# One encoder layer: result stores on ScalarE's and GpSimd's queues, three larger result tiles, and h2 blocks stored without norm_mlp's factors

## The chip, the cores and the metric

The kernel runs on one core of a Trainium2 chip. The time is the device time of one execution in microseconds (us). TensorE (PE) does the matmuls, with PEld for its weight loads; VectorE is DVE, ScalarE is ACT, GpSimd is POOL, and SyncE (SP) issues DMAs. Each of them works through its own list of instructions in order.

## The reference

One layer of an encoder: a norm, an input projection, two kinds of attention, gates and an output projection, and a feed-forward part with squared ReLU, all in fp32, for 2048 tokens of 1024 features.

```python
h = rms_norm(x, norm_mix[l])
z = h @ w_in[l]                      # 1024 x 4352
q_a, k_a, v_a, q_b, k_b, v_b, g_a, g_b = jnp.split(z, offsets, axis=-1)
y_a = windowed_gqa(...)              # |t-s| <= 128, ALiBi, sink
y_b = neighborhood_attn(...)         # 8 x 16 window on a grid of 64 columns
y = sigmoid(g_a + b) * (y_a @ w_proj_a) + sigmoid(g_b + b) * (y_b @ w_proj_b)
x = x + y @ w_out
h2 = rms_norm(x, norm_mlp[l])
x = x + relu(h2 @ w_up) ** 2 @ w_down
...
return rms_norm(x, norm_final)
```

## The kernel before, in words

Every fp32 operand of a large product is split into a high and a low part (a cast by ACT, a subtraction by DVE: L280 and L281), and a product is three matmuls, high x high, high x low, low x high (L200 to L202, L284 to L286). The large projections go in *quads*: two blocks of tokens by two blocks of features, computed with seven block products in place of eight, so operands and results pass through sums and differences on DVE (L277).

The program has these stages, in the order of time of the profile:

- **Input projection, up to about 380 us.** Nine quads (QUADS, L548). `in_quad` and `in_seeded` evict the results of each product from PSUM into tiles of the ring `zc` (ten tiles of 128x512) or, for q and k, as high and low part into the ring `ze` (two tiles of 128x2x512). `in_result` (L440) stores them: q and k to `qs_*` and `ks_*` (L450), v to `vs_*` (L458), the gates to `zg` (L461). All go on SP's queue.
- **Beside it, the parts of W_out.** In the third, fourth, eighth and ninth quad, a generator `wo_parts` (L663 to L690) makes the seven sums of W_out's blocks, splits each into `hi` (a `zc` tile) and the low part (in place, in a `zv` or `xin` tile), and stores both to `wo_d` (L677). One step of it runs after each product of the quad (`next(prep)`, L723). In the sixth and seventh quad two blocks of normalised x are transposed by DVE into `ze` tiles and stored to `h1d` (`turned_out`, L239).
- **Windowed attention A (about 380 to 700 us)**, which reloads `h1d` (`h_pages`, L743: `raw<-h1d`, four loads a block, hT by ACT and DVE) for the q, k and v of the last two blocks of tokens. It needs the table `dist` (L793), from which POOL makes the bias tiles `biasa` (L799), and loads of `ka`, `va`, `qa`.
- **Neighbourhood attention B (about 700 to 1075 us).**
- **Gated projection and W_out (about 1075 to 1410 us)**: `gated` and `out_products`; the parts of W_out come back as `pgl<-wo_d`. The results are normalised rows; `turned_out` transposes them, multiplies by norm_mlp's factors (`gain`, L252) and stores four pieces of 32x8x128 for each of four groups to `h2d`. Blocks 0 and 1 go through `ht` tiles earlier; blocks 2 and 3 come last, through the two tiles `m` and the four tiles `hu` (`turned_last`, L1456).
- **Up projection (about 1410 to 2030 us)**: `up_right` makes the seven right-hand pages (`ubh1` to `ubh7`) of h2, `ahead` and `parts_ahead` prepare those of the second half (blocks 2 and 3) in small chunks, `up_quad` does the products. The pages lie where tiles of the stage before lay, so a page waits until `m` or `hu` is stored.
- **Down projection and the final norm, to the end.**

Nearly every DMA is on SP's queue, in program order: 1364 rows of SP's list. A DMA whose data is not ready, whose target is not free, or whose semaphore (eight are shared in turn by the DMAs of SP and ACT) is still in use holds up all behind it. Before the change POOL issues no DMA, and ACT 48 (32 of `zg`, in the attention, and 16 of `x2d`). The order on each engine is made by a scheduler from the program's dependences, so an edit in one place also shifts rows elsewhere.

Of the kernel before, what the change touches and what calls it, by code (L numbers as in the profile page):

```python
# [8 lines left out]
F32 = mybir.dt.float32  # L9
F32R = mybir.dt.float32r  # L10
AF = mybir.ActivationFunctionType
# [81 lines left out]
def encoder_layer(ctx, tc, x, norm_mix, w_in, b_gate, sink, rpb, w_pa, w_pb, w_out,  # L93
# [12 lines left out]
    def pools(stack, side, tags, name):  # L106

        return {t: pool(f"{name}_{t}", side=side, stack=stack) for t in tags}
# [130 lines left out]
    def turned_out(d, ht, tiles, g, gain=None, queue=None):  # L239

        hv = ht.rearrange("p (j t c) -> p t j c", j=8, t=4)
        for t in range(4):
            V.transpose(out=hv[:, t], in_=tiles[t][:, g * 256 : (g + 1) * 256].rearrange("p (j c) -> p j c", j=8))
        h3 = ht.rearrange("p (j x) -> p j x", j=8)
        if gain is not None:
            (step, n), _ = gain.ap  # L250
            gv = bass.AP(gain.tensor, gain.offset + 8 * g, [[step, n], [1, 8], [0, P]])
            V.tensor_tensor(out=h3, in0=h3, in1=gv, op=ALU.mult)  # L252
        dv = d.rearrange("(j i) (a x) -> a i j x", i=32, a=4)
        for a in range(4):
            (queue or SY).dma_start(dv[a][:, 8 * g : 8 * g + 8], h3[32 * a : 32 * a + 32])
# [36 lines left out]
    def ring(stack, tag, shape, dt, bufs, side="right"):  # L292

        pl = pool(f"r_{tag}", side=side, stack=stack)
        return lambda: T(pl, shape, dt, tag, bufs)
# [25 lines left out]
    in_sum = ring(s_z, "zS", [P, 4, 256], F32, 2)  # L321
    in_v2 = [ring(s_z, "zv2", [P, 1024], F32, 1)]
    in_page[5] = ring(s_z, "zh5", PAGE, F32R, 2)
    in_c = ring(s_z, "zc", [P, BT], F32, 10)
    in_e = ring(s_z, "ze", [P, 2, BT], F32, 2)
    in_whl = ring(s_z, "zwhl", [P, 2, 4, 256], F32R, 3)
    in_page[3] = ring(s_z, "zh3", PAGE, F32R, 2)
    s_kv = ExitStack()
# [117 lines left out]
    def in_result(col, b, src, in_psum):  # L446

        if col < O_VB and col != O_VA:
            for dst, t in qk_parts(col, b, src, in_e()):
                SY.dma_start(dst, t)  # L450
            return
        if in_psum:
            t = in_c()
            A.copy(t, src)
            src = t
        if is_v(col):
            for dst, t in v_parts(col, b, src, zbank(tpool, 2), in_v2[-1]()):
                SY.dma_start(dst, t)  # L458
        else:
            f = (col - O_GA) // P  # L460
            SY.dma_start(zg[b][0][f // 8, (f % 8) * P : (f % 8 + 1) * P, :], src)  # L461

    def in_quad(c, w, lf, right, ybanks=ypool, zbanks=zpool):

# [198 lines left out]
    def wo_parts(k, own):  # L663

        rows = [own(), own()]
        for p, r in enumerate(rows):
            SY.dma_start(r, w_out[0][(4 * p + k) * P : (4 * p + k + 1) * P, :])
        yield
        b11, b12, b21, b22 = (r[:, j * BT : (j + 1) * BT] for r in rows for j in range(2))
        t1, t3 = (t[:, j * BT : (j + 1) * BT] for t in (own(),) for j in range(2))  # L670

        def part(n, src):
            hi = in_c()
            A.copy(hi.bitcast(F32R), src)
            V.tensor_tensor(out=src.bitcast(F32R), in0=src, in1=hi, op=ALU.subtract)
            for z, t in enumerate((hi, src)):
                SY.dma_start(wo_d[n][k // 2, k % 2][:, z], t)  # L677

        add(V, t1, b12, b11, ALU.subtract)
        yield  # L680
        add(V, t3, b22, b12, ALU.subtract)
        part(1, b11)
        yield
        add(V, b12, b22, t1, ALU.subtract)
        part(3, b22)
        yield
        add(V, b11, b21, b12, ALU.subtract)
        for n, src in ((2, b21), (5, t1), (7, t3), (6, b12), (4, b11)):
            part(n, src)
            yield  # L690
# [9 lines left out]
    for q in range(2, len(QUADS)):  # L700
        prep = iter(())
        if q in (2, 3):
            prep = wo_parts(q - 2, own_v)
        elif q in (7, 8):
            prep = wo_parts(q - 5, own_x)
        next(prep, None)
        if q == 5:
            s_v.close()
            in_v2.pop()
            xp = pools(s_z, "right", ("xin", "st"), "x2")  # L710
        if q == 7:
            bias_tables()
        lf = list(in_left(ws, 256, (1, 2) if q == 2 else (), ORDER if q == 2 else ORDER_3))
        if q + 1 < len(QUADS):
            ws = in_weights(*QUADS[q + 1])
        if q in (5, 6):

            b = q - 3
            xt = x_tiles(xp, b, 3)
            normalised(xp, xt, Junk(), by_scalar=True)  # L720
        ops2.extend(lf if q == 2 else ())
        for n, _ in enumerate(quad2 if q == 2 else in_seeded(*QUADS[q], iter(lf), right)):
            next(prep, None)  # L723
            if q in (5, 6) and n < 4:
                turned_out(h1d[b - 2], in_e().rearrange("p k x -> p (k x)"), xt, n)
        for _ in prep:
            pass
# [388 lines left out]
    p4x["st"] = cp  # L1116
    gain = turned_gain(T(p4x, [P, P], F32, "gt", 1), norm_mlp)
    next(first_y)

    n_bank = [0]  # L1120

# [76 lines left out]
    h2p_d = {n: [dp.tile([BT, BT], F32, name=f"h2part{n}{z}") for z in range(2)] for n in (1, 5)}  # L1198
    stored = [None]

    def parts_ahead(n):

        src = h2d[2] if n == 1 else h2s_d[n]
        for k in range(4):
            lo, hi = up_rings["chunk"](), up_rings["chunk"]()
            with tc.issue_after(stored[0]) if k == 0 and stored[0] else nullcontext():
                SY.dma_start(lo, src[k * P : (k + 1) * P, :])
            yield
            A.copy(hi.bitcast(F32R), lo)
            V.tensor_tensor(out=lo.bitcast(F32R), in0=lo, in1=hi, op=ALU.subtract)  # L1210
            for z, t in enumerate((hi, lo)):
                SY.dma_start(h2p_d[n][z][k * P : (k + 1) * P, :], t)

    def ahead(k):

        b = {}
        for j, p in ((0, 0), (1, 0), (1, 1), (0, 1)):
            b[p, j] = up_rings["chunk"]()
            with tc.issue_after(stored[0]):
                SY.dma_start(b[p, j], h2d[2 + j][p * BT + k * P : p * BT + (k + 1) * P, :])  # L1220
        t1, t3, t2, t4 = b[0, 0], b[0, 1], b[1, 1], b[1, 0]
        for n, out, x, y in ((5, t1, t3, t1), (7, t3, t2, t3), (6, t2, t2, t1), (4, t4, t4, t2)):
            yield
            add(V, out, x, y, ALU.subtract)
            SY.dma_start(h2s_d[n][k * P : (k + 1) * P, :], out)
# [3 lines left out]
    def up_right(m):  # L1229

        right = {}

        def block(b, j, p):
            SY.dma_start(b, h2d[2 * m + j][p * BT : (p + 1) * BT, :].rearrange("(k p) t -> p k t", p=P))
            return b

        def parts(n, src):
            hi, lo = up_page[n](), up_page[n]()
            for s, h, l, e in zip(halves(src), halves(hi), halves(lo), (V, V)):
                last = split(s, h, l, e)  # L1240
            right[n] = (hi, lo)
            page_done[0] = last

        def less(out, a, c):
            for o, x, y in zip(halves(out), halves(a), halves(c)):
                add(V, o, x, y, ALU.subtract)

        def made(n):
            b = up_rings["raw"]()
            SY.dma_start(b, h2s_d[n].rearrange("(k p) t -> p k t", p=P))  # L1250
            return b

        def loaded(n):
            right[n] = up_page[n](), up_page[n]()
            for t, d in zip(right[n], h2p_d[n]):
                SY.dma_start(t.bitcast(F32), d.rearrange("(k p) t -> p k t", p=P))

        if m:
            yield
            loaded(1)  # L1260
            loaded(5)
            parts(6, made(6))
            yield right
            parts(2, block(up_rings["raw"](), 0, 1))
            parts(7, made(7))
            parts(4, made(4))
            parts(3, block(up_rings["rb"](), 1, 1))
            return
        b11 = block(up_rings["raw"](), 0, 0)
        yield  # L1270
        b12 = block(up_rings["raw"](), 1, 0)
        t = up_rings["raw"]()
        less(t, b12, b11)
        parts(1, b11)
        parts(5, t)
        yield
        b22 = block(up_rings["raw"](), 1, 1)
        less(b12, b22, b12)
        less(t, b22, t)
        parts(6, t)  # L1280
        yield right
        b21 = block(up_rings["rb"](), 0, 1)
        parts(2, b21)
        yield right
        parts(7, b12)
        less(b21, b21, t)
        parts(4, b21)
        parts(3, b22)
# [167 lines left out]
    def turned_last(i, own):  # L1456

        for g in range(4):
            turned_out(h2d[2 + i], own(g), rows[i], g, gain)

    state = {"y": next_y}
    rows = None
# [273 lines left out]
```

## Time and profile before

| | us |
|---|---|
| median of 3 runs | 2660.17 (2657.42 to 2662.54) |
| profiled execution | 2664.86 |
| its span | 2663.0 |
| PE busy | 2584.8 |
| DVE busy | 1635.8 |
| ACT busy | 1274.8 |
| POOL busy | 348.5 |

The mean granted clock of TensorE was 0.991. The views used below: the page's busy times; the waits of an engine (who was waited for, in total, how often, the longest); windows (busy time of each engine in a stretch, with the number of instructions, then the granted clock, the DMA engines' busy share and GB/s); the chain of waits (start, length, what: followed back from the end of the stretch, each step to what released it); timelines of one engine (start, length, instruction). SPq, ACTq and the like are queues: the time of issuing a DMA. A DMA row in the chain is the time from issue to landing. A line number can be that of a helper.

### The profile page before, as it was taken

The page shows a single profiled execution, that of the slowest core. Times are in us where ns is not written, and L with a number is a line of the kernel's source. Part 1 is how long each engine was busy: PE and PEld are TensorE (multiplying, and loading weights), DVE is VectorE, ACT ScalarE, POOL GpSimd, SP SyncE. Part 2 cuts the span into 40 slices and gives each one's busy share as a digit, 9 for nine tenths or more (in the row PEclk, how much of TensorE's full clock was granted, in tenths as well). Part 3 has the DMA queues.
Part 4 walks back from the last instruction along what each step waited for, and adds up shares of the span by engine and source line. Part 5 has one row for each costly group of instructions (what it writes and reads, how often), then busy time and mean ns, then how long its engine had stood idle before and what let it go on. Part 6 is the DMA issues. An engine that isn't in the chain of part 4 may idle for free.

```text
span 2663.0 us, 34440 instructions
## 1 busy us (share of the span) xinstructions
PE 2584.8 (97%) x12044; PEld 2143.4 (80%) x12044; DVE 1635.8 (61%) x2619; ACT 1274.8 (48%) x2291; POOL 348.5 (13%) x433
## 2 busy tenths in 40 slices
PE   7989989999999999999998999999999999999998
PEld 6878767787888888878876888888887888888887
DVE  7855556665544445465678676776565634555766
ACT  7445446666555556344245444554444332322444
POOL 0000014334465552000000000000000000000011
PEclk9999998999999999999998999999999999999999
DMA  5777695446777664776677655854436935445555
GB/s 182 255 215 216 202 293 144 117 111 172 208 214 214 173 192 135 263 235 223 222 276 246 213 194 196 294 202 154 146 115 256 332 107 181 143 146 169 185 192 167
DMA packets 351725, 525.93 MB, mean 197 GB/s; under 512 B 28584, under 2 KB 172072, under 8 KB 349376
## 3 DMA queue, kind: packets, MB, share of 16 engines
q1 hardware_dynamic: 344640, 506.95, 60.2%
q10 hardware_dynamic: 6912, 16.78, 1.7%
q8 instruction: 95, 1.56, 0.2%
q14 instruction: 78, 0.64, 0.1%
HBM read 349.51 MB, written 174.13 MB: 197 GB/s over the span
## 4 chain that ended last, share of the span: by engine, by line
PE 78%; DMA 9%; DVE 7%; ACT 2%; issue 2%; SPq 1%; POOL 0%; POOLq 0%; ACTq 0%; DVEq 0%
PE b L285 15%; PE b L284 15%; PE b L286 15%; PE mm L200 4%; PE mm L201 4%; PE mm L202 4%; PE av L1029 2%; PE b L200 2%; PE b L201 2%; PE b L202 2%; PE pt L1018 2%; PE s L990 2%; PE zb L286 1%; PE zb L284 1%; PE zb L285 1%
## 5 line engine op out<-in xcount | busy, mean ns | idle before, releaser
L285 PE MATMUL b<-dwh,dah 128*128 128x512 f32 x896 | 349.0, 390 | 0.4 <-DVE dwh L281 0.4
L286 PE MATMUL b<-dwh,dah 128*128 128x512 f32 x896 | 348.1, 389 | 0.0
L284 PE MATMUL b<-dwh,dah 128*128 128x512 f32 x896 | 338.2, 389 | 1.7 <-ACT dwh L280 1.7
L280 ACT CAST dah<-da 128x1024 fp32r<-128x1024 f32 (+1 forms) x128 | 120.8, 945 | 367.5 <-PE b L286 245.3
L281 DVE TENSOR_TENSOR dah<-da,dah 128x1024 fp32r<-128x1024 f32 (+1 forms) x128 | 139.3, 1090 | 226.2 <-ACT dah L280 224.6
L284 PE MATMUL b<-ubh,uwhlb 128*128 128x512 f32 x592 | 233.0, 394 | 11.8 <-ACT ubh L280 6.9
L285 PE MATMUL b<-ubh,uwhlb 128*128 128x512 f32 x592 | 233.2, 394 | 0.6 <-DVE ubh L281 0.5
L286 PE MATMUL b<-ubh,uwhlb 128*128 128x512 f32 x592 | 231.9, 393 | 0.0
L200 PE MATMUL mm<-hT,whl 128*128 128x512 f32 x544 | 219.8, 404 | 4.6 <-ACT hT L753 4.6
L201 PE MATMUL mm<-hT,whl 128*128 128x512 f32 x544 | 215.5, 396 | 0.3 <-DVE hT L754 0.3
L202 PE MATMUL mm<-hT,whl 128*128 128x512 f32 x544 | 215.6, 396 | 0.0
L284 PE MATMUL zb<-zh,zwhl 128*128 128x512 f32 x476 | 187.6, 394 | 11.8 <-ACT zb L523 7.3
L284 PEld LDWEIGHTS b<-dwh,dah 128*128 128x128 f32 x896 | 168.2, 188 | 36.8 <-ACT dwh L280 2.1
L285 PEld LDWEIGHTS b<-dwh,dah 128*128 128x128 f32 x896 | 168.3, 188 | 35.6 <-DVE dwh L281 0.8
L286 PEld LDWEIGHTS b<-dwh,dah 128*128 128x128 f32 x896 | 168.3, 188 | 34.8
L286 PE MATMUL zb<-zh,zwhl 128*128 128x512 f32 x476 | 186.1, 393 | 2.2 <-DVE zwhl L281 2.2
L285 PE MATMUL zb<-zh,zwhl 128*128 128x512 f32 x476 | 187.1, 393 | 0.0
L277 DVE TENSOR_TENSOR uc<-b,uc 128x512 f32<-128x512 f32 x160 | 109.2, 689 | 124.2 <-PE b L286 117.8
L284 PEld LDWEIGHTS b<-ubh,uwhlb 128*128 128x128 f32 x592 | 112.6, 190 | 36.7 <-ACT ubh L280 7.7
L285 PEld LDWEIGHTS b<-ubh,uwhlb 128*128 128x128 f32 x592 | 112.4, 190 | 25.2 <-DVE ubh L281 1.7
L286 PEld LDWEIGHTS b<-ubh,uwhlb 128*128 128x128 f32 x592 | 112.6, 190 | 23.5
L200 PEld LDWEIGHTS mm<-hT,whl 128*128 128x128 f32 x544 | 103.0, 189 | 23.2 <-ACT hT L753 5.2
(264 smaller groups left out, 5809.3 us busy)
## 6 DMA issues: line engine op xcount, KB each, us to landing
at<-uc SPq DMA_DIRECT2D x224, 256.0 KB
da<-at SPq DMA_DIRECT2D x96, 512.0 KB
dw<-in_w_down_dram SPq DMA_DIRECT2D x160, 256.0 KB
uraw<-in_w_up_dram SPq DMA_DIRECT2D x32, 1024.0 KB
pgl<-wo_d SPq DMA_DIRECT2D x28, 1024.0 KB
raw<-in_w_in_dram SPq DMA_DIRECT2D x34, 512.0 KB
zraw<-in_w_in_dram SPq DMA_DIRECT2D x16, 1024.0 KB
z<-zg SPq DMA_DIRECT2D x64, 256.0 KB
```

The costliest lines, as they stand in the source:

```text
L200: PE.matmul(ps, lh, rh, start=first, stop=False)
L201: PE.matmul(ps, lh, rl, start=False, stop=False)
L202: PE.matmul(ps, ll, rh, start=False, stop=last)
L277: return eng.tensor_tensor(out=out, in0=a, in1=b, op=op).ins
L280: A.copy(hi, src)
L281: return eng.tensor_tensor(out=lo, in0=src, in1=hi.bitcast(F32), op=ALU.subtract).ins
L284: PE.matmul(ps, lh, rh, start=first, stop=False, skip_group_check=True)
L285: PE.matmul(ps, lh, rl, start=False, stop=False, skip_group_check=True)
L286: PE.matmul(ps, ll, rh, start=False, stop=last, skip_group_check=True)
L990: PE.matmul(ps[:, :n], q[:, i, :], kv[:, z, B_R0[i] // 4 : (B_R0[i] + B_NR[i]) // 4, 4 * B_C0[j] : 4 * (B_C0[j] + w)], start=z == 0, stop= ...
L1018: PE.transpose(pt[:kp, at + (i - i0) * P : at + (i - i0 + 1) * P], s[i][:, rr : rr + kp], ident)
L1029: last = PE.matmul(po[:, i0 * P : (i0 + ni) * P], v[:kp, c, :], src[:kp, o : o + ni * P], start=first, stop=(c == 7 and z == 1), skip_grou ...
```

## The change

- The stores of the high parts of `wo_d` move from SP to ACT's queue, those of the low parts to POOL's: 28 each. The 32 gate stores of L461 move to ACT (the 16 whose tile ACT has copied from PSUM) and to POOL (the other 16).
- The ring `zc` has nine tiles in place of ten, `ze` three in place of two. The small tiles `st` of the sixth quad and later lie in another pool.
- In the ninth quad two steps of `wo_parts` run after each product.
- `turned_last` stores blocks 2 and 3 of h2 on POOL's queue, and without the multiplication by the factors (eight DVE instructions on 128x1024). In its place the factors are multiplied in by ACT where these blocks are read in the up projection (`by_gain`): 4 times in `parts_ahead(1)`, 16 in `ahead`, 8 in `up_right(1)`, each on 128x512. They are loaded again for this, from norm_mlp, into the tile `g_mix`.

```diff
-    in_c = ring(s_z, "zc", [P, BT], F32, 10)
-    in_e = ring(s_z, "ze", [P, 2, BT], F32, 2)
+    in_c = ring(s_z, "zc", [P, BT], F32, 9)
+    in_e = ring(s_z, "ze", [P, 2, BT], F32, 3)
...
-            SY.dma_start(zg[b][0][f // 8, (f % 8) * P : (f % 8 + 1) * P, :], src)
+            (A if in_psum else G).dma_start(zg[b][0][f // 8, (f % 8) * P : (f % 8 + 1) * P, :], src)
...
-            for z, t in enumerate((hi, src)):
-                SY.dma_start(wo_d[n][k // 2, k % 2][:, z], t)
+            for z, t, queue in ((0, hi, A), (1, src, G)):
+                queue.dma_start(wo_d[n][k // 2, k % 2][:, z], t)
...
-            xp = pools(s_z, "right", ("xin", "st"), "x2")
+            xp = {**pools(s_z, "right", ("xin",), "x2"), "st": cp}
...
-            next(prep, None)
+            for _ in range(2 if q == 8 else 1):
+                next(prep, None)
...
+    with nc.allow_non_contiguous_dma(reason="small per-feature vectors"):
+        SY.dma_start(g_mix, norm_mlp[0].rearrange("(k p) -> p k", p=P))
...
+    def by_gain(t, k):
+        A.activation(t, t, AF.Copy, scale=g_mix[:, k : k + 1])
...
+            if n == 1:
+                by_gain(lo, k)
             A.copy(hi.bitcast(F32R), lo)
...
                 SY.dma_start(b[p, j], h2d[2 + j][p * BT + k * P : p * BT + (k + 1) * P, :])
+            by_gain(b[p, j], 4 * p + k)
...
             SY.dma_start(b, h2d[2 * m + j][p * BT : (p + 1) * BT, :].rearrange("(k p) t -> p k t", p=P))
+            if m:
+                for k in range(4):
+                    by_gain(b[:, k], 4 * p + k)
...
-            turned_out(h2d[2 + i], own(g), rows[i], g, gain)
+            turned_out(h2d[2 + i], own(g), rows[i], g, queue=G)
```

What this does to the lists, at three places. First SP in the third and fourth quad; `zraw` are weights of the next quad, in two halves, `ks_b` stores of k. Before:

```order
L677 DMA wo_d_928<-zc_1460 128x512
L677 DMA wo_d_928<-zv_123_1167 128x512
L450 DMA ks_b_88<-ze_1316 64x2x512 x2
L677 DMA wo_d_926<-zc_1465 128x512
L677 DMA wo_d_926<-zv_123_1167 128x512
L450 DMA ks_b_89<-ze_1333 64x2x512 x2
L553 DMA zraw_1499<-in_w_in_dram 128x4x512
L349 DMA zv_197_1830<-in_x_dram 32x1024 x4
```

After, the same place of SP's list:

```order
L553 DMA zraw_1497<-in_w_in_dram 128x4x512
L450 DMA ks_b_88<-ze_1316 64x2x512 x2
L553 DMA zraw_1499<-in_w_in_dram 128x4x512
L450 DMA ks_b_89<-ze_1333 64x2x512 x2
L450 DMA ks_b_90<-ze_1357 64x2x512 x2
L349 DMA zv_197_1827<-in_x_dram 32x1024 x3
```

The wo_d stores are gone from SP, and the second half of the weights stands behind one pair of ks_b stores in place of two pairs and the wo_d stores.

Second, SP at the start of the windowed attention, before:

```order
L677 DMA wo_d_928<-zc_2981 128x512
L677 DMA wo_d_926<-zc_2986 128x512
L677 DMA wo_d_928<-xin_2716 128x512
L677 DMA wo_d_926<-xin_2716 128x512
L810 DMA ka_329_3115<-ks_a_80 64x1024
L811 DMA ka_329_3115<-ks_a_80 64x1024
L187 DMA raw_4070<-in_w_in_dram 128x8x128
L187 DMA raw_4132<-in_w_in_dram 128x8x128
L812 DMA va_331_3117<-vs_a_82 128x1024
L187 DMA raw_4209<-in_w_in_dram 128x8x128
L773 DMA ks_a_81<-z_4097 64x2x512
L793 DMA dist_3113<-in_dist_a_dram 128x384
```

The wo_d stores, the next weights and a store of ks_a stand ahead of `dist` there. After:

```order
L751 DMA raw_3130<-h1d_97 128x2x512
L810 DMA ka_329_3111<-ks_a_80 128x1024
L751 DMA raw_3138<-h1d_97 128x2x512
L811 DMA ka_329_3111<-ks_a_80 64x1024
L812 DMA ka_329_3111<-ks_a_80 64x1024
L751 DMA raw_3144<-h1d_97 128x2x512
L794 DMA dist_3109<-in_dist_a_dram 128x384
L187 DMA raw_4066<-in_w_in_dram 128x8x128
```

`dist` now follows the last load of h1d, ahead of the next weights and of the ks_a store.

Third, SP at the passage from W_out to the up projection (`pgl` are W_out's parts, `urb` and `uraw` blocks of h2 and weights of the up projection, `at` its results). Before:

```order
L1385 DMA pgl_13279<-wo_d_926 128x2x1024
L255 DMA h2d_10827<-m_1576_13336 32x8x128 x8
L255 DMA h2d_10827<-m_1577_13337 32x8x128 x8
L1234 DMA urb_13490<-h2d_10825 128x4x512
L1154 DMA uraw_13594<-in_w_up_dram 128x4x512
L255 DMA h2d_10828<-hu_13517 32x8x128 x4
```

The rest of the 16 stores out of `hu` follows, then a store of `at` and the next load of `uraw`. After, SP there:

```order
L1397 DMA pgl_13276<-wo_d_926 128x2x1024
L1243 DMA urb_13483<-h2d_10821 128x4x512
L1157 DMA uraw_13583<-in_w_up_dram 128x4x512
L1157 DMA uraw_13585<-in_w_up_dram 128x4x512
L1157 DMA uraw_13855<-in_w_up_dram 128x4x512
L1318 DMA at_0_10877<-uc_13685 128x512
```

The 32 stores stand in POOL's list instead, four small instructions of a norm between the two blocks (the list is cut off at the second of these four; the 16 stores out of `hu` follow the fourth):

```order
L228 TENSOR_TENSOR st_13264<-st_13264,power 128x1
L255 DMA h2d_10823<-m_1576_13333 32x8x128 x8
L255 DMA h2d_10823<-m_1577_13334 32x8x128 x8
L228 TENSOR_TENSOR st_13423<-st_13423,power 128x1
L228 TENSOR_TENSOR st_13430<-st_13430,power 128x1
```

The list of PE is the same up to the up projection, where the first quad takes page 2 ahead of page 6 (24 matmuls each); before it was the other way round. Page 2 lies where the first `m` tile lay, page 6 needs both `m` tiles stored, page 7 the `hu` tiles. On DVE the low part of page 2 stands before the transposes into `hu` after the change, that of page 6 between those of the second and the third row tile.

## The prediction

> **What bounds the kernel now.** I read the page first, then the time that TensorE (PE) waits, then busy time by stretch, then the chain of waits at the three places that stand out.
>
> ```profile
> PE 2584.8 (97%) x12044; PEld 2143.4 (80%) x12044; DVE 1635.8 (61%) x2619; ACT 1274.8 (48%) x2291; POOL 348.5 (13%) x433
> ```
>
> PE is busy 97% of a span of 2663.0 us, and the change takes no matmul away. So a gain can come only from PE's idle time and from stretches at a lower granted clock. These are PE's waits that lie where the change works (engine, line waited at, releaser: total, times, longest):
>
> ```profile
> PE zb L284 <- ACT zb L523: 7.3, 1, 7.3
> PE b L284 <- ACT ubh L280: 6.9, 2, 5.7
> PE mm L200 <- ACT hT L753: 4.6, 1, 4.6
> PE b L284 <- DVE uc L277: 3.3, 1, 3.3
> ```
>
> The view by stretches adds the clock (busy time of PE, PEld, DVE, ACT, POOL; granted clock; DMA share; GB/s):
>
> ```profile
> 100.00:150.00 50.00, 50.00 (x222) 41.43 (x221) 37.59 (x49) 24.09 (x37) 0.00 (x0) 1.00 0.90 289
> 150.00:200.00 50.00, 42.21 (x180) 34.11 (x179) 28.71 (x32) 20.07 (x26) 0.00 (x0) 0.93 0.64 193
> 350.00:400.00 50.00, 42.15 (x174) 32.12 (x172) 23.27 (x37) 19.14 (x31) 10.38 (x10) 0.93 0.99 320
> 400.00:450.00 50.00, 45.88 (x216) 37.76 (x216) 32.80 (x104) 33.62 (x102) 20.46 (x35) 0.87 0.58 150
> 1400.00:1450.00 50.00, 42.27 (x165) 32.85 (x164) 41.69 (x65) 27.66 (x41) 3.71 (x5) 0.91 0.78 224
> 1450.00:1500.00 50.00, 46.68 (x197) 38.12 (x196) 35.08 (x41) 23.08 (x33) 0.00 (x0) 0.95 0.67 233
> ```
>
> The first row is a healthy stretch: 50 of 50 us at clock 1.00. In the others the loss is idle time plus 50 x (1 - clock). Place B (150 to 200): 7.8 + 3.5 = 11.3 us. Place C (350 to 450): 7.9 + 4.1 + 3.5 + 6.5 = 22.0. Place E (1400 to 1500): 7.7 + 3.3 + 4.5 + 2.5 = 18.0. Together 51 us, the most that a cure of all three could bring. In these rows the clock is low only where PE had gaps, so I let it go with the gap.
>
> **Place B.** SP's timeline and then the chain of waits there (start, length, what):
>
> ```profile
> 152.94 1.23 SPq L450 DMA_DIRECT2D ks_b<-ze  x2
> ...
> 156.60 1.23 SPq L450 DMA_DIRECT2D ks_b<-ze  x2
> 157.88 0.96 SPq L553 DMA_DIRECT2D zraw<-in_w_in_dram  x1
> ```
> ```profile
> 157.88 10.35 DMA zraw<-in_w_in_dram
> ...
> 170.82 1.11 ACT ze L425
> ...
> 173.72 3.57 DMA ks_b<-ze
> ...
> 177.38 1.07 ACT ze L425
> ...
> 180.22 0.79 PE zb L284
> ```
>
> SP stands in stores, and the second half of the next weights (zraw) is issued only at 157.88; its arrival frees DVE, then ACT's ze. The second ze then waits for the store of an earlier one out of a ring of two, from 171.9 to 177.4. In the new SP order this load stands ahead of the second pair of ks_b stores and of all wo_d stores, and the ring has three tiles.
>
> - Load: it can follow the first ks_b pair, which left from 152.94 to 154.17, so about 154.2 in place of 157.9: 3.7 us.
> - Ring: the first ze ended at 171.93, the second began at 177.38: 5.4 us.
>
> 9.1 us of release stand against a gap of 7.3, so the gap should close and the clock with it. What is late next is DVE, still full. I take -10 of 11.3; ends: 0 (a new wait takes the place) and -11.3.
>
> **Place C.** Here the windowed attention begins:
>
> ```profile
> 376.04 7.49 DMA raw<-h1d
> ...
> 389.45 1.44 SPq L773
> ...
> 390.94 5.57 DMA dist<-in_dist_a_dram
> ...
> 396.66 0.12 POOL biasa L799
> ...
> 398.61 7.15 DMA qa<-qs_a
> ```
>
> The last h1d page takes 7.49 us to land while the DMA engines are at 0.99; the dist table is issued behind a store of ks_a that waits for DVE; then qa. After the change dist follows the last h1d load directly (376 + 1 instead of 390.9), and the wo_d and zg stores that filled this stretch leave when they are ready. The bytes are the same, so some crowding stays: of the 4.6 us of hT I take half (2.3), of the waits for dist, bias and qa (the rest of 12.0 us of idle time, 7.4) 3, of the 10.0 us of clock 5. That is -10; ends 0 and -22.
>
> **Place E.** SP's own queue (start, length of all, instruction) and the chain:
>
> ```profile
> 1406.93 14.96 SPq L255 DMA_DIRECT2D h2d<-m  x16
> 1431.11 10.27 SPq L255 DMA_DIRECT2D h2d<-hu  x16
> ```
> ```profile
> 1409.78 1.13 DVE m L252
> ...
> 1421.40 2.62 DMA h2d<-m
> 1424.08 1.05 ACT ubh L280
> ...
> 1438.29 2.83 DMA h2d<-hu
> ...
> 1442.23 8.27 DMA uraw<-in_w_up_dram
> ...
> 1456.42 0.61 DVE uc L277
> ```
>
> The up projection's pages lie in the memory of m and hu and wait until these are stored; and an up weight that stands behind the 16 hu stores is issued at 1442.23, which makes the last stall (DVE uc, 3.3 us). The change clears SP: the weights go out directly after the last W_out load. The eight multiplies by the factors (L252, 1.13 us each here) leave DVE. But GpSimd (POOL) must now issue the 32 stores, and no row of before shows a store from its queue. The nearest rows:
>
> ```profile
> L255 SPq DMA_DIRECT2D h2d<-hu x16: 303/478/1232, 1431.1 to 1440.7; - x16
> L173 ACTq DMA_DIRECT2D x2d<-xr x16: 326/326/1334, 1223.5 to 1415.1; - x16
> L228 POOL TENSOR_TENSOR st<-st,power x32: 547/548/1517, 6.2 to 1423.5; 128x1 f32<-128x1 f32 x32
> L177 POOL TENSOR_TENSOR whl<-raw,whl 128x1024 fp32r<-128x1024 f32 x34 | 81.4, 2396 | 175.3 <-ACT whl L176 167.4 <-PE av L854 4.4 <-PE pt L848 3.5
> ```
>
> Per store: at least 0.3 us (SP, the same store), at most POOL's dearest row, 2.4. Nearest, I think, is the same store's median on SP plus one small instruction of POOL's: 0.48 + 0.55, about 1.0.
>
> When PE wants the pages: of its 6.9 us for ubh the shorter wait was 1.2 (6.9 - 5.7) and ended with the ACT ubh of 1424.08, so the first of the three pages is wanted at 1424; a product on one page is 24 matmuls, 5.4 us at the 222 in 50 us of the healthy row; so the second is wanted at 1429.3, the third at 1434.7. The new order takes first the page that needs eight m stores, then the one that needs all 16, then hu's; and DVE turns the last hu tiles behind the second page's low part.
>
> At 1.0 us the m stores run from about 1404 (among their transposes, which end before the L252 quoted) to 1420. With 2.6 us to land, 1.05 for ACT and 1.13 for DVE, the first page is there at 1416.8, the second at 1424.8: in time. The hu stores start when the last hu transposes end, which came 1428.8 before:
>
> ```profile
> 1427.43 1.41 DVE L247 STREAM_TRANSPOSE hu<-xr 128x256 f32<-128x256 f32 x4
> ```
>
> From 1428.5 they run to 1444.5, land 2.83 later and are through ACT at 1448.4: 13.7 us late, and 3.4 of clock. That is 17.1 in place of 18: I take -1. So here the stall only changes its owner, and the price of one POOL store decides, 16 times over. Ends: at 0.3 us the page is 2.5 us late, -15; at 2.4 us the three pages stall 4 + 14 + 38 us, the clock takes some 10 more, +48.
>
> The Trainium skill ("DMA: Bandwidth & Descriptors", the list of facts and the section SWDGE vs HWDGE vs iDMA) puts the first byte of a DMA from GpSimd at about 1 us against 0.6 for SP or ScalarE; by that figure alone the last landing would be 0.4 us later and the sum above 0.4 us worse; no row of before shows one.
>
> **What the change adds.**
>
> - ScalarE issues 44 more stores (28 wo_d high parts, 16 zg) at 0.33 us from the ACTq row: 14.5 us between 100 and 380 us, where this view shows ACT with room:
>
> ```profile
> 100.00:400.00 300.00, 282.44 (x1234) 229.49 (x1232) 178.22 (x238) 140.28 (x217) 19.25 (x24) 0.98 0.78 239
> 1450.00:2030.00 580.00, 575.06 (x2527) 475.59 (x2526) 393.29 (x472) 280.05 (x393) 0.00 (x0) 1.00 0.54 188
> ```
>
>   ACT is busy 140 of 300 us, so the issue time itself is hidden. But ACT works in order, and a store that waits for one of the DMA semaphores holds the evictions of PSUM behind it, and PE behind these. The same row's longest issue was 1.33 us, 1.0 over its median; four such on the path: +4. Ends 0 and 44 x 1.0 = 44.
> - POOL issues 44 more in the same stretch, 44 us at 1.0, with 19 of 300 us busy: hidden until 380; a tile whose store is late comes free late, which I count in the +4.
> - One zc tile less: the 40 users of the ring pass more quickly once stores no longer queue on SP; 0.
> - 28 multiplies by the factors on ScalarE in the up projection, 128x512 each, as the row L1295 of the same shape:
>
> ```profile
> L1295 ACT ACTIVATE uc<-uc 128x512 f32<-128x512 f32 x122 | 76.0, 630 | 3.0
> ```
>
>   28 x 0.63 = 17.6 us, ACT busy 280 of 580 us there: hidden, but for an eviction that finds up to four of them (2.5 us) ahead. +2, ends 0 and 10 (four such places).
> - The reload of the factors: one small load on SP near 400 us, behind loads; under 1 us; 0.
> - Two steps of preparation per product in the last quad move the wo_d stores earlier: counted at C.
>
> **Sum.** -10 - 10 - 1 + 4 + 2 = -15 us against the profiled execution's 2664.86, that is 2650. This execution stood 4.7 us over the median of 2660.17, which I take as its own scatter, so on the runs: 2660.2 - 15 = 2645 us, 0.6% less. A change under 0.2% (5.3 us) can hardly be told from none.
>
> **Rivals.**
>
> 1. *POOL's stores are dear: slower.* At 1.5 us each the second page is 3.5 us late and the third 24, with 5 of clock 32 in place of 18: +14, which eats B, C and the costs (-14). So it decides from 1.5 us. At 2 us the pages come at 1424.8, 1440.8 and 1478: 1 + 11 + 32 us and 9 of clock, 53: +35 and a sum of +20, 2680. For it: each store writes 256 rows of 512 B, and DVE is busy 41.69 of 50 us there. Against: POOL's small instruction at 0.55. The Trainium skill ("SBUF — State Buffer", Who interferes with whom) says that DVE in its two-port modes keeps GpSimd from writing descriptors, though DVE's two-input operations do not; no run here shows it. Chance 0.14.
> 2. *POOL's stores are cheap.* At 0.5 us the hu page is there at 1440.4, 5.7 late with 1.7 of clock: E -10.6, the sum -25: 2635. For it: SP issues the same store in 0.48. Chance 0.20.
> 3. *Nothing is gained.* In the in-projection ACT's in-order stores wait where SP's did, or the full DMA engines (0.90 at 100 to 150, 0.99 at 350 to 400) keep B and C as they are: the gain of 20 shrinks to 5, and -5 - 1 + 6 = 0: 2660. The Trainium skill ("DMA: Bandwidth & Descriptors", Issuing engines are not separate DMA queues) has the rule: several issuing engines save only the time of issuing. The trace speaks against it at B, where the load was late by its place in SP's queue. Chance 0.13.
> 4. *B and C go wholly*: -33 - 1 + 6 = -28, 2632. Chance 0.05.
>
> **How the numbers follow.** The forecast (POOL at 0.8 to 1.2 us, so E from -5 to +5: 2638 to 2652 for it alone) 0.45; with rivals 2 and 4 faster 0.70. Rival 3: same 0.13. Rival 1 0.14, and 0.03 for a stall I don't see: slower 0.17. The range leaves out the upper half of rival 1, and below it goes past rivals 2 and 4 to where both come together (-28 - 10 = 2622): 2622 to 2680.
>
> **What would show it.** Right: no gap at 173 to 180; dist issued before 380; no PE wait for DVE uc near 1455, but one for ACT ubh of 10 to 15 us near 1440; POOL's row for a store near 1.0 us. Wrong: POOL's row at 1.5 us or more, or at 0.5; new PE waits for ACT evictions between 100 and 380; PE waits for ACT uc in the up projection above 4 us.

## The result, and the profile after

The changed kernel takes 2662.32 us (median of 12 runs, 2657.24 to 2668.39), the kernel before 2661.63 (12 runs, 2657.42 to 2666.60). The ratio is 1.0003, 95% interval 0.9992 to 1.0014: no change that can be measured, where 2645 was forecast. The three places tell why. This is the view by stretches of the changed kernel, columns as in the prediction:

```profile
150.00:200.00 50.00, 47.85 (x218) 39.12 (x218) 34.93 (x40) 24.16 (x30) 2.70 (x5) 1.00 0.75 227
350.00:400.00 50.00, 45.15 (x200) 33.92 (x198) 28.44 (x84) 26.98 (x75) 21.04 (x32) 0.97 0.95 285
400.00:450.00 50.00, 47.49 (x242) 39.54 (x242) 33.09 (x87) 31.22 (x83) 17.61 (x26) 0.97 0.50 141
1400.00:1450.00 50.00, 19.48 (x74) 14.25 (x73) 28.56 (x38) 20.40 (x23) 16.86 (x27) 0.74 0.58 163
1450.00:1500.00 50.00, 49.71 (x217) 40.69 (x216) 30.90 (x38) 27.59 (x42) 0.00 (x0) 0.99 0.61 210
```

Read as before (idle time of PE plus 50 x (1 - clock)), place B loses 2.2 us in place of 11.3, place C 4.9 + 2.5 + 1.5 + 1.5 = 10.4 in place of 22.0, and place E 30.5 + 0.3 + 13.0 + 0.5 = 44.3 in place of 18.0. So -9.1, -11.6 and +26.3.

The third of these is too large, because a low clock costs PE time only while PE works. In the changed kernel the clock stood at half for 27.3 us, and PE was busy for 4.3 of them:

```profile
1423.50:1450.80 27.30, 4.28 (x9) 2.98 (x10) 9.65 (x9) 3.88 (x4) 7.56 (x13) 0.50 0.62 165
```

So those 13 us of clock are about 2; the rest is counted twice, as idle time and as clock. A count of matmuls avoids this. Both kernels run 12044 of them, so one can compare when the same number has begun. These are the views from the start to four moments, the kernel before first, then the changed one:

```profile
0.00:1350.00 1350.00, 1296.22 (x6401) 1080.20 (x6402) 796.12 (x1529) 712.70 (x1462) 328.55 (x408) 0.99 0.67 201
0.00:1507.00 1507.00, 1440.50 (x7001) 1196.41 (x7002) 918.17 (x1690) 788.05 (x1573) 333.90 (x416) 0.99 0.68 205
```
```profile
0.00:1330.58 1330.58, 1288.98 (x6401) 1073.38 (x6402) 794.30 (x1529) 712.38 (x1462) 355.03 (x452) 1.00 0.68 203
0.00:1502.98 1502.98, 1429.24 (x7001) 1186.56 (x7002) 906.74 (x1681) 791.06 (x1580) 379.43 (x492) 0.99 0.67 205
```

The same 600 matmuls take 157.0 us before and 172.4 after. Counted like this, the three places are:

| place, matmuls | before, us | after, us | difference |
|---|---|---|---|
| B, 611 to 821 | 149.8 to 206.2 | 150.1 to 198.5 | -8.0 |
| C, 1451 to 1901 | 350.0 to 464.6 | 339.6 to 442.8 | -11.4 |
| E, 6401 to 7001 | 1350.0 to 1507.0 | 1330.6 to 1503.0 | +15.4 |

Together that is -4.0, and the spans of the two profiled executions (2663.0 and 2658.9 us) differ by -4.1. The losses by stretches of the experiments below are read the first way, so they too are somewhat high where PE had a long gap.

One wait holds most of the loss at E. From the changed kernel's view of PE's waits (total, times, longest):

```profile
PE b L284 <- ACT ubh L280: 27.4, 2, 26.5
PE mm L200 <- ACT hT L754: 2.6, 2, 2.1
```

The 7.3 us of ACT zb are gone from that view, the 3.3 us of DVE uc are 0.3, the 4.6 us of hT are 2.6, and ubh has risen from 6.9 to 27.4. GpSimd's timeline shows where the 26.5 us come from (start, length, what, in brackets the idle time ahead of it):

```profile
1406.59 0.58 POOL L255 DMA_DIRECT2D h2d<-m  x1 [0.70 <-issue]
1407.19 3.42 POOL L228 TENSOR_TENSOR st<-st,power 128x1 f32<-128x1 f32 x4
1417.86 1.78 POOL L255 DMA_DIRECT2D h2d<-hu  x3 [7.24 <-DVE hu L247]
1424.36 1.78 POOL L255 DMA_DIRECT2D h2d<-hu  x3 [4.73 <-issue]
1432.94 1.88 POOL L255 DMA_DIRECT2D h2d<-hu  x3 [6.79 <-issue]
1437.37 1.74 POOL L255 DMA_DIRECT2D h2d<-hu  x3 [2.54 <-issue]
1440.12 0.58 POOL L255 DMA_DIRECT2D h2d<-hu  x1 [1.02 <-issue]
1441.01 1.17 POOL L255 DMA_DIRECT2D h2d<-hu  x2 [0.30 <-issue]
1442.79 0.58 POOL L255 DMA_DIRECT2D h2d<-hu  x1 [0.62 <-issue]
```

One store costs GpSimd 0.58 us, about half of the 1.0 I had taken. But they leave in threes, with pauses in which the engine has nothing to do. The time from issue to landing of the first three, of the next three and of those from 1432.9 (minimum, median, maximum):

```profile
DMA to landing us min/median/max: 5.7/5.9/6.2
```
```profile
DMA to landing us min/median/max: 8.2/8.3/8.3
```
```profile
DMA to landing us min/median/max: 3.5/3.7/4.1
```

The first store left at 1417.86 and landed 6.2 us later, at 1424.06; the fourth left at 1424.36. The fourth landed at 1432.63, the seventh left at 1432.94. Over most of the 32 stores of the two blocks, one leaves 0.31 us after the store three places before it has landed, the others right behind their neighbour, and never are more than three in flight. The hu block so takes from 1417.86 to 1443.37, 25.5 us, where SP needed 10.3 before; at the end stands the page, here the subtraction for its low part, after 17.3 us of idle time on DVE:

```profile
1446.46 2.36 DVE L281 TENSOR_TENSOR ubh<-uraw,ubh 128x1024 fp32r<-128x1024 f32 x2 [17.31 <-ACT ubh L280]
```

Two more things are visible. The four small norm instructions of the hu rows (L228) stand in GpSimd's list behind the m stores and run only at 1407 to 1411, so the last transposes into hu end at 1418.4. And stores land in 2.4 us at best, in 8.3 at worst; while the hu stores are out, SP issues the next weights:

```profile
1413.55 9.41 SPq L1157 DMA_DIRECT2D uraw<-in_w_up_dram  x3
```

### The profile page after: what moved, and what is told of

The parts are those of the page before. It is cut to its first block, busy times and chain, and to the rows that moved or that the text cites. A ratio compares the mean times of both kernels' runs of the same rounds, so it can differ in the third digit from the quotient of the medians.

```text
span 2658.9 us, 34486 instructions
## 1 busy us (share of the span) xinstructions
PE 2573.6 (97%) x12044; PEld 2132.8 (80%) x12044; DVE 1624.8 (61%) x2611; ACT 1290.3 (49%) x2319; POOL 394.0 (15%) x509
## 5 line engine op out<-in xcount | busy, mean ns | idle before, releaser
L286 PE MATMUL b<-dwh,dah 128*128 128x512 f32 x896 | 347.8, 389 | 0.0
L284 PE MATMUL b<-ubh,uwhlb 128*128 128x512 f32 x592 | 231.3, 391 | 29.0 <-ACT ubh L280 27.4
L286 PE MATMUL b<-ubh,uwhla 128*128 128x512 f32 x304 | 118.1, 389 | 1.9 <-DVE uwhla L281 1.9
```

Source lines behind the costliest of these rows:

```text
L284: PE.matmul(ps, lh, rh, start=first, stop=False, skip_group_check=True)
L286: PE.matmul(ps, ll, rh, start=False, stop=last, skip_group_check=True)
```

## The experiments

All ratios are to the kernel before, run on the same chip beside the experiment, with 95% intervals.

**Theories.** Theory 1: the change is two independent things, a gain of some 20 us before 450 us and a loss as large at the h2 stores on GpSimd. Theory 2: gains early are given back later, whatever stands there. Theory 3: at the passage it is the omitted factors and the new order of pages that cost, not GpSimd.

### The two halves apart

a_inproj has the changed rings, queues and steps of the input projection, and `turned_last` as before:

```diff
-            turned_out(h2d[2 + i], own(g), rows[i], g, queue=G)
+            turned_out(h2d[2 + i], own(g), rows[i], g, gain)
```

and no `by_gain`. 

> Only the first half of the change: the stores of the W_out parts and of the gates on ScalarE's and GpSimd's queues, the rings of nine and three tiles, two steps of preparation in the last quad. The last h2 blocks leave as before, with the factors, on SP. Theory 1 (two independent effects: the input projection and the start of the attention gain about 21 us, the h2 stores on GpSimd lose about as much): 2638 to 2643 us, PE's losses between 150 and 200 and between 350 and 450 us as small as in the changed kernel (about 2 and 10 us), those at the passage to the up projection about 18 us as before. Theory 2 (what is gained early is given back later whatever stands there, for instance through the granted clock): within 5 us of 2660.

Measured: 2643.83 us, ratio 0.9921 (0.9901 to 0.9941), just above the range of theory 1.

b_h2pool is the kernel before with the diff's second half alone (`queue=G`, no factors at the store, `by_gain` in the up projection). 

> Only the second half of the change, on the kernel before: blocks 2 and 3 of h2 stored on GpSimd's queue without the factors, ScalarE multiplies by them in the up projection. Theory 1: slower by 20 to 27 us, 2680 to 2688, with one wait of PE for ACT ubh of 20 us or more near 1445 us, and with at most three of these stores in flight. Theory 2: about 2660.

Measured: 2682.36 us, ratio 1.0071 (1.0056 to 1.0086), with the wait of theory 1:

```profile
PE b L284 <- ACT ubh L280: 25.1, 2, 24.2
```

-0.8% and +0.7% add up to the whole change's 0.0%. Theory 2 falls: nothing is given back, two effects of opposite sign meet.

### The h2 stores on other queues

c_h2sp is the whole change, with `turned_out(h2d[2 + i], own(g), rows[i], g)`, so the stores are on SP. 

> The whole change, but the last h2 blocks leave on SP's queue (still without the factors). Theory 1: the loss at the passage falls from about 44 us to 10 to 18, since up to eight stores are in flight on SP and landing is all that a store waits for: 2630 to 2642 us. If instead it is the later place of the factors or the new order of the pages that makes the stall (theory 3), the wait for ACT ubh stays above 15 us and the time is near 2660.

Measured: 2639.45 us, ratio 0.9909 (0.9894 to 0.9924). The wait for ubh is 4.3 us:

```profile
PE b L284 <- ACT ubh L280: 4.3, 1, 4.3
```

Without the factors the passage is better than before, so that half of theory 3 falls. The other half, the order of the pages, is not settled by this run: with the stores on SP the scheduler goes back to the order of before. In the program page 2 is made from `urb` and page 6 from `uraw`. These are the low parts of the first page that is made behind the m stores, in the changed kernel and then in c_h2sp:

```profile
1402.28 2.36 DVE L281 TENSOR_TENSOR ubh<-urb,ubh 128x1024 fp32r<-128x1024 f32 x2 [6.08 <-DMA h2d<-m]
```
```profile
1403.30 2.36 DVE L281 TENSOR_TENSOR ubh<-uraw,ubh 128x1024 fp32r<-128x1024 f32 x2 [4.31 <-ACT ubh L280]
```

So what is shown here is that the stores on GpSimd, together with the order that comes with them, make the loss. j_m_pool_hu_sp below keeps the changed order.

d_h2act puts them on ScalarE (`queue=A`). 

> The whole change, but the last h2 blocks leave on ScalarE's queue. Theory 1: 32 issues of 0.33 us, no limit of three in flight, and the up weights are not held up on SP: the loss at the passage falls to 5 to 12 us, 2625 to 2636 us. Theory 3 (factors, order of the pages): wait for ACT ubh above 15 us, near 2660. A third outcome: ScalarE's stores in order hold up its own casts of the pages, then the wait is for ACT but with ScalarE standing in its queue, 2640 to 2650.

Measured: 2649.87 us, ratio 0.9944 (0.9929 to 0.9959). It is the third outcome in kind, and as dear. The order of the pages is again that of before. ScalarE's timeline:

```profile
1386.74 9.34 ACTq L255 DMA_DIRECT2D h2d<-m  x16
1396.17 2.47 ACTq L173 DMA_DIRECT2D x2d<-xr  x4
1398.69 0.63 ACT L223 ACTIVATE junk<-xr 128x512 bf16<-128x512 f32 x1 [14.30 <-DMA h2d<-m]
```

16 issues take 9.34 us there, 0.58 each, not the 0.33 I had expected; the norms of the hu rows wait 14.3 us behind them and four stores of x2d, and PE in the end 17.4 us for ubh.

j_m_pool_hu_sp leaves m's stores on GpSimd and puts hu's on SP (`queue=(G, SY)[i]`). 

> The whole change, but the stores out of hu leave on SP's queue; those out of m stay on GpSimd's. If the loss comes from the hu stores alone: as with all on SP, 2637 to 2642. If it comes in part from the m stores, behind which four small norm instructions of the hu rows stand in GpSimd's list (they ran at 1407 to 1410 us in the changed kernel, right after the last m store): the transposes into hu come some 5 us later than with all on SP, a wait for ACT ubh of 9 to 12 us, 2645 to 2650.

Measured: 2648.38 us, ratio 0.9939 (0.9923 to 0.9956), a wait for ubh of 12.1 us. The order of the pages is that of the changed kernel here, and still hu's stores on SP are worth 14 us (2662 to 2648): so for this part the queue is the cause, at the same order. The other 9 us, against c_h2sp, are the m stores on GpSimd with the order that comes with them: the four norms run at 1408.0, right behind the last m store, and the last transposes into hu end at 1419.2 in place of 1409.4. But DVE, too, has other work ahead of these transposes, from 1403.6 to 1410.4 without a pause. Which of the two, late norms or new order, costs the 9 us was not tried apart.

i_m_sp_hu_act has m's on SP and hu's on ScalarE. 

> The whole change, but m's stores leave on SP's queue and hu's on ScalarE's. So GpSimd's norms for the hu rows stand behind nothing, and the up weights behind the m stores alone. If ScalarE has room for 16 issues there, the hu stores are out some 10 us after their transposes, as on SP, and the weights come earlier: 2634 to 2639 us. If ScalarE's issues hold up its casts and evictions, as with both on ScalarE (where it issued for 10.2 us without a break): 2640 to 2648.

Measured: 2641.25 us, ratio 0.9919 (0.9902 to 0.9935), a wait for ubh of 7.7 us; that is in the second range, and no better than SP for both. The order of the pages is that of before.

### Why a GpSimd store was slow

g_split cuts each store into two of half the rows:

```diff
-            (queue or SY).dma_start(dv[a][:, 8 * g : 8 * g + 8], h3[32 * a : 32 * a + 32])
+            for j in (0, 4) if queue else ():
+                queue.dma_start(dv[a][:, 8 * g + j : 8 * g + j + 4], h3[32 * a : 32 * a + 32, j : j + 4])
```

> The changed kernel, but each of the 32 h2 stores on GpSimd's queue is cut into two of half the rows (32x4x128, 128 runs of 512 B). In the changed kernel a store leaves 0.31 us after the store three before it has landed. If the limit is three stores in flight whatever their size, the 32 half stores of hu take at least 32/3 x 2.7 = 29 us and with the landing times seen there some 50, so 20 to 30 us more than the changed kernel: 2680 to 2690. If the limit is a number of rows (768 fit, 1024 don't), six half stores are in flight and the block takes about what it took: 2655 to 2670, with a half store leaving after the landing of the one six before it.

Measured: 2661.38 us, ratio 0.9988 (0.9979 to 0.9997), the time of the changed kernel. Its GpSimd timeline:

```profile
1424.15 9.54 POOL L256 DMA_DIRECT2D h2d<-hu  x17 [8.69 <-DVE hu L247]
1434.76 0.55 POOL L256 DMA_DIRECT2D h2d<-hu  x1 [1.08 <-issue]
1437.44 0.55 POOL L256 DMA_DIRECT2D h2d<-hu  x1 [2.13 <-issue]
```

17 half stores leave without a pause; the 18th leaves at 1434.76, 0.31 us after the 11th, issued at 1429.76, has landed (4.69 us). So at most seven of 128 rows are in flight, 896 rows, against three of 256, 768. A count of three is out; a limit on rows below 1024 fits both, since neither four whole stores nor eight halves ever were in flight. What exactly holds these rows no run shows. The halves gain nothing in all, because each costs 0.55 us to issue, as much as a whole one.

h_weights_late makes the next weights wait on SP for the hu stores, by a small load of their result ahead of them:

```diff
+                seen = SY.dma_start(sink_t[0:1, 0:4], h2d[3][BT - 1 : BT, BT - 4 : BT])
...
-                ws = up_weights(q + 1)
+                with tc.issue_after(seen.ins) if m == 0 and q == 0 else nullcontext():
+                    ws = up_weights(q + 1)
```

> The changed kernel, but the next weights of the up projection are issued on SP only after the last hu store has landed (a small load of the last four values of h2, into a tile no longer used, stands ahead of them). If the weights' transfers are what makes a store take 4 to 8 us to land in place of 2.4 to 2.8, the 16 hu stores now take about 16 x 2.9 / 3 = 15.5 us in place of 25.5, the stall falls by about 10 us and its clock by 5: 2645 to 2652. If landing is slow for another reason, the stores still take 25 us and the weights come later besides: 2660 to 2675.

Measured: 2658.75 us, ratio 0.9979 (0.9970 to 0.9988), in neither range. The load I had chosen reads the piece that the eighth of the 16 stores writes, so the weights went out at 1427.98, in the middle of them. That made the test within one run: the ten stores that left before this landed after 2.4 to 3.9 us, the six after it after 4.9 to 6.2.

o_weights_later takes the last row (`h2d[3][2 * BT - 1 : 2 * BT, ...]`). 

> As the run in which the next weights wait for the hu stores, but they wait for the 16th of these, not for the eighth. There, stores that left before the weights landed after 2.4 to 3.9 us, those behind them after 4.9 to 6.2. So now all 16 should land in 2.4 to 3.9, leave in 15 to 17 us in place of 25.5, and the stall fall to 16 to 19 us: 2648 to 2655 us. If the slow landing had another cause, as there: 2658.

Measured: 2652.18 us, ratio 0.9962 (0.9947 to 0.9977). All 16 land in 2.4 to 4.3 us:

```profile
DMA to landing us min/median/max: 2.4/2.6/4.3
```

They leave in 16.0 us (1420.1 to 1436.1) in place of 25.5, and the wait for ubh is 17.0 in place of 26.5. So some 10 us of the loss are the weights' transfers, which the change itself let out earlier; the rest is the three in flight, and what comes with the m stores on GpSimd.

### What gave the gain before 450 us

k_rings is c_h2sp with the old rings (ten zc, two ze). 

> The change with h2 on SP, but with the rings as before (ten zc, two ze tiles). If the third ze tile closes the gap at 173 us, the gap comes back with 4 to 7 us and 3 of clock: 7 to 10 us slower than the run with h2 on SP, 2645 to 2651. If the stores off SP's queue close it, 2637 to 2642.

Measured: 2644.61 us, ratio 0.9924 (0.9908 to 0.9939). The gap at B is back, with gates and W_out parts off SP, and larger than before (7.3):

```profile
PE zb L284 <- ACT zb L523: 8.6, 1, 8.6
```

n_rings_only is the kernel before with only the rings changed (the tiles `st` move to the other pool with them). 

> The kernel before with nothing but the rings of nine zc and three ze tiles. If the ring of two ze tiles is what made the 7.3 us gap at 173 us (5.4 us of it were a wait for a ze tile's store), the gap falls to about 2 us without its 3.4 us of clock: 2651 to 2656, the rest as before. If the stores on SP's queue are needed as well: 2658 to 2663.

Measured: 2650.88 us, ratio 0.9957 (0.9942 to 0.9972). B is closed with all stores on SP:

```profile
150.00:200.00 50.00, 49.05 (x223) 39.73 (x222) 35.12 (x39) 23.98 (x30) 0.00 (x0) 1.00 0.75 227
350.00:400.00 50.00, 39.22 (x163) 29.11 (x161) 25.16 (x62) 20.61 (x54) 12.35 (x18) 0.93 1.04 316
```

The second half of the weights left no earlier than in the kernel before (157.88 there):

```profile
157.95 0.86 SPq L553 DMA_DIRECT2D zraw<-in_w_in_dram  x1
```

C is not closed: 10.8 + 3.5 in this stretch, and 4.1 in the next.

l_wo_sp is c_h2sp with the W_out parts back on SP (`queue` is SY for both). 

> The change with h2 on SP, but the stores of the W_out parts on SP's queue as before; gates and rings as changed. The run with the old rings showed that the third ze tile closes most of the gap at 173 us, so that place should stay small (1 to 5 us); if the crowd of late stores between 360 and 400 us comes from the W_out stores waiting in SP's queue, 5 to 10 us come back there: 2645 to 2650. If the gates alone made the crowd: 2638 to 2643.

Measured: 2633.91 us, ratio 0.9889 (0.9874 to 0.9904), under both ranges. Not slower but, if anything, faster than c_h2sp: moving the W_out parts was no gain. The two intervals overlap.

p_rings_gates and r_rings_wo add to n_rings_only the gate stores on ScalarE and GpSimd, or those of the W_out parts. 

> The kernel before with the rings of nine zc and three ze tiles and the gate stores on ScalarE's and GpSimd's queues; W_out parts and h2 as before. If the gates' stores are what stands ahead of the loads at the start of the attention: PE's losses between 350 and 450 us fall from the 18 us of the rings alone to about 8, 2640 to 2643 us. If it is the W_out parts: 2649 to 2653, as with the rings alone.

Measured: 2652.48 us, ratio 0.9961 (0.9947 to 0.9974).

> The kernel before with the rings of nine zc and three ze tiles and the stores of the W_out parts on ScalarE's and GpSimd's queues; gates and h2 as before. If the W_out parts make the crowd at 350 to 450 us: 2640 to 2643 us. If they don't, 2649 to 2653; and if moving them costs something by itself, up to 2656.

Measured: 2653.46 us, ratio 0.9972 (0.9961 to 0.9982). Neither group of stores does anything for C; it loses 21.7 and 22.1 us in these runs. I had expected one of them to be the cause, and both were not.

What no run had yet had alone was the second step of preparation. s_rings_prep adds it to n_rings_only:

```diff
-            next(prep, None)
+            for _ in range(2 if q == 8 else 1):
+                next(prep, None)
```

> The kernel before with the rings of nine zc and three ze tiles and two steps of the preparation of W_out per product in the last quad; every store on SP as before. If the second step is what empties the start of the attention (the W_out parts are made and stored some products earlier): the losses between 350 and 450 us fall from 18 to about 8 to 11 us, 2640 to 2645 us. If moved stores are needed for that: 2649 to 2653.

Measured: 2638.63 us, ratio 0.9916 (0.9901 to 0.9931), somewhat better than expected. The second step is the cause at C, with every store on SP:

```profile
350.00:400.00 50.00, 46.78 (x209) 35.34 (x208) 30.30 (x86) 27.98 (x76) 17.89 (x26) 0.97 0.95 283
400.00:450.00 50.00, 49.21 (x259) 41.17 (x258) 33.14 (x93) 32.12 (x90) 20.96 (x32) 1.00 0.55 151
```

3.2 + 0.8 + 1.5 = 5.5 us. The third ze tile is not needed for it: with the old rings and the second step, in k_rings, C loses 4.7 us. The casts of the W_out parts of the last quads, in the kernel before and in this one (minimum, median, maximum ns, first and last start):

```profile
L674 ACT CAST zc<-xin x14: 617/622/624, 303.5 to 373.0; 128x512 fp32r<-128x512 f32 x14
```
```profile
L674 ACT CAST zc<-xin x14: 610/621/624, 294.5 to 347.8; 128x512 fp32r<-128x512 f32 x14
```

Before, the last cast started at 373.0, in the midst of C; now it is at 347.8, and SP comes to `dist` at 362.72 in place of 390.94:

```profile
362.72 0.34 SPq L794 DMA_DIRECT2D dist<-in_dist_a_dram  x1
```

t_no_queues is the change without any moved store: rings, second step, no factors at the store, all on SP. 

> The change without any moved store: rings, two steps per product in the last quad, the last h2 blocks without the factors (ScalarE multiplies later), all stores on SP's queue. If no moved store is needed: 2632 to 2640 us, as with gates moved (2634). If the gates' queues give a part: 2642 to 2648.

Measured: 2630.88 us, ratio 0.9882 (0.9866 to 0.9899), the fastest of all and a little better than expected, 1.2% under the kernel before. Its three places lose 1.3, 4.6 and 8.5 us:

```profile
150.00:200.00 50.00, 48.72 (x221) 39.52 (x221) 33.80 (x37) 22.84 (x29) 0.00 (x0) 1.00 0.74 228
350.00:400.00 50.00, 46.22 (x213) 34.91 (x212) 31.17 (x85) 27.65 (x76) 18.74 (x26) 1.00 0.98 287
400.00:450.00 50.00, 49.23 (x260) 41.12 (x259) 33.23 (x95) 32.22 (x88) 21.02 (x32) 1.00 0.56 151
1400.00:1450.00 50.00, 43.00 (x180) 34.18 (x179) 45.26 (x54) 30.78 (x42) 0.00 (x0) 0.97 0.75 244
```

So of the change's three parts the one that is its largest, the queues, is worth nothing before 450 us, and its h2 stores cost some 23 us after (2662 against the 2639 of c_h2sp). The Trainium skill ("DMA: Bandwidth & Descriptors", Issuing engines are not separate DMA queues) says that issuing from several engines saves only the issuing time, usually little; these runs agree, with 2651, 2652 and 2653 us for the rings alone, with the gates and with the W_out parts moved.

## Why the prediction was wrong, point by point

- **Place E** was forecast at -1 and came to +15.4: the step that failed. I multiplied the time of issuing one GpSimd store by 16. That time was 0.58 us, not 1.0, and so near the 0.5 of rival 2, which should have been faster; but what holds the next store is the landing of the one three before, 2.4 us at best and up to 8.3 beside the weights. 25.5 us for 16 stores are 1.6 us each, just past the 1.5 from which rival 1 said that the place eats the rest. So rival 1 had the place, the threshold and nearly the loss (+14 at 1.5 us); its mechanism, a dear issue, was not the one. The rule of the Trainium skill that I named there ("SBUF — State Buffer", Who interferes with whom) was not needed: GpSimd's time for a store stayed at 0.58 to 0.68 us with DVE at work.
- **Left out at E**: what the change lets out earlier. I counted the weights going out directly behind the last W_out load as a gain of 3.3 us; they made the stores land later and cost some 10 (o_weights_later). And in GpSimd's list the norms of the hu rows stand behind the m stores, which the order shows and I did not price: with the new order of the pages, 9 us of the time by j_m_pool_hu_sp.
- **Place B** was forecast at -10 and came to -8.0, but one of its two steps was wrong. The ring step (5.4 us) holds: n_rings_only closes the gap by the ring alone. The load step was not needed: there the load left as late as before, at 157.95, and with the old rings, and gates and W_out parts off SP (k_rings), the gap was 8.6 us. In the changed kernel the load left at 156.59 against 157.88, 1.3 us earlier and not 3.7: SP stood 13.7 us ahead of the ks_b stores, for DVE.

```profile
154.86 1.53 SPq L450 DMA_DIRECT2D ks_b<-ze  x2
156.59 1.16 SPq L553 DMA_DIRECT2D zraw<-in_w_in_dram  x1
```

- **Place C** was forecast at -10 and came to -11.4, for the wrong reason; that the size fits is luck. I read the late `dist` and the crowd as SP's queue being full of stores and let the second step of preparation count for nothing of its own ("counted at C"). The runs show the reverse: moved stores alone change nothing, the second step with all stores on SP takes C to 5.5 us. The row that would have said it was in the profile before: the last cast of a W_out part at 373.0, so its stores could not leave sooner from any queue.
- **The factors** (+2) have the other sign. t_no_queues against s_rings_prep, which differ in the factors alone, is 7.8 us less. That DVE is free of eight instructions where pages are waited for, and that ScalarE's 28 multiplies are hidden, fits this; PE's wait for ACT uc of 1.6 us in the up projection is as before.
- **ScalarE's stores in order** (+4): no run has this term by itself. What is new with the W_out parts moved is a wait of PE for DVE (zc) near 156 us, 2.2 us in the changed kernel and 1.9 in r_rings_wo, at most 0.5 in n_rings_only and p_rings_gates; why DVE is late there was not followed. c_h2sp against l_wo_sp is +5.5 us, but there the parts leave both queues, and the intervals overlap.
- **The sum**: B and C were forecast at -20 and came to -19.4. E, forecast at -1, came to +15.4. The +4 and +2 of costs did not show beside these three places. That gives -4 for the two profiled executions, in place of -15, and the miss is E's. The medians are +0.7 us apart; the 5 us between that and -4 are within the scatter of single executions (2657 to 2668).
- **Two readings of the prediction itself.** Its losses count the low clock also where PE stood idle, so the 51 us of the three places are a little high. And in its rivals the hu stores start some 6 us after the last m store, a term for which it gives no row; in the changed kernel they started 10.7 us after it (1407.17 to 1417.86).

## What to carry to other kernels

Before moving stores to another queue, ask when their data is ready: work that is made late is stored late from any queue, and making it one step earlier or giving its ring one more tile is the change that pays. A queue is priced not by its issue time alone but by how many of its transfers may be in flight and how long each takes to land beside what else is then let out. And what stands behind the moved instructions in the new engine's list, here four tiny norms, belongs in the sum, as does the order that the scheduler then makes on the other engines.

## What the runs showed of the hardware

- From GpSimd's queue at most three stores of 256 rows of 512 B, or seven of 128 rows, were in flight at once (the changed kernel, g_split); where the engine had to wait, the next left 0.31 us after the landing of the one three (or seven) places before.
- GpSimd's own time for a store was 0.54 to 0.58 us in the median, whatever its size (128 rows of 2 KB, 128 of 512 B or 256 of 512 B); on ScalarE the 256-row store took 0.49 us in the median and 16 in a row 9.3 to 10.2, against 0.33 for the W_out parts.
- The same 128 KB store landed after 2.4 us at best and after up to 8.3 us (9.8 in b_h2pool) beside loads of 1 MB; with the next weights held back until all 16 had landed, after 2.4 to 4.3 (o_weights_later).
- A gap of PE of 26.5 us left TensorE's clock at half for 27.3 us, of which PE worked 4.3 (the changed kernel).
